# RoPE and per-head scores on one core: which loads of q GpSimd issues around DMA engine 4

## The chip, the cores and the metric

The kernel runs on one core of a Trainium2 chip. The metric is device time in microseconds (us), the median of several executions; a profile of one further execution shows where the time lies. A core has TensorE (PE; its weight loads are listed as PEld), VectorE (DVE), ScalarE (ACT), GpSimd (POOL) and SyncE (SP, which only issues DMAs here), and 16 DMA engines that move data between HBM and the core's SBUF.

## The reference

q and k have 16 batches of 512 positions, 16 heads and 64 values, in float32. Each is rotated by its position's cos and sin, and then the scores of every pair of positions are taken, per batch and head:

```python
q_rot = np.concatenate([q1 * cos_q - q2 * sin_q, q1 * sin_q + q2 * cos_q], axis=-1)
k_rot = np.concatenate([k1 * cos_q - k2 * sin_q, k1 * sin_q + k2 * cos_q], axis=-1)
scores = np.einsum('bshd,bthd->bsht', q_rot, k_rot)
```

The inputs are 67 MB together, the output is 268 MB.

## The kernel before

Position s of a batch lies at partition s // 4 and chunk s % 4, so a batch of q or k is a tile of 128 partitions by 16 KB, and each partition's 16 KB are contiguous in HBM. A step handles one chunk of q of one batch: 64 steps, i = 0 to 63, four per batch. In a step, for each of eight pairs of heads p, TensorE multiplies the transposed q chunk with the batch's transposed k (`scores`, line 392), ScalarE copies the result from PSUM into a stage tile (line 418), and after the eighth pair SP stores the stage, 4 MB, in one DMA (line 427, recorded in the profile at line 237, that of the helper `dma`). There are three stages; a stage is filled again when its store has landed. Between the pairs TensorE transposes the q chunk of the next step and the k chunk of the step four later (`transposed`, line 349), and VectorE rotates q two steps ahead and k five steps ahead (`rope`, line 312). The first batch is treated in smaller pieces and stored in 16 DMAs of 1 MB.

q and k have two input buffers each, so batch b of q uses the buffer of batch b - 2. Its load is placed at the end of step i with i % 4 == 2, as batch i // 4 + 2 (lines 507 and 508): the load of q13 at the end of step 46, q14 of step 50, q15 of step 54. k's load follows at the end of the next step, two batches and more ahead (k15 at the end of step 51). After the load of q15, in step 54, nothing is left to load, and steps 55 to 63 only store.

Every operation is added to a plan (`Plan.add`), which works out the semaphore waits, and each engine's queue holds its operations in the plan's order. SP's queue thus holds stores and loads in the order of the steps, each behind the one before it.

`load` (line 264) has two forms. A plain load is one DMA of 128 partitions issued by SP. The batches listed in `RELIEVED` (line 260) are loaded in another way: GpSimd resets the cursor of its own DMA queue (line 107), moves it by a tiny DMA (`move_cursor`, line 282) of 5 rows, so that the next transfer begins behind engine 4 (`SLOW`), and then issues a load of the first 120 partitions (`halves`, line 289), which is meant for the other 15 engines, eight partitions each in two pieces of 8 KB a partition. The last 8 partitions depend on the entry's number x. With x even, SP loads them by a DMA of 8 rows, a row to each of eight engines, engine 4 among them. With x odd, GpSimd loads them first, with a cursor moved by 8, so that they are meant for the other eight engines. GpSimd has no other work after the start, so its queue waits only for the input buffer to be free: until VectorE and TensorE have read batch b - 2 to its end.

The function that the diff touches holds the whole kernel; its part around the change is the dictionary `RELIEVED` and `load`, and the loop over the steps calls it.

Of the kernel before, what the change touches and what calls it, by code (L numbers as in the profile page):

```python
# [178 lines left out]
def kernel(  # L179
# [56 lines left out]
    def dma(engine, e, dst, src, sem, reads=(), writes=(), also=()):  # L236
        plan.add(engine, one(lambda: e.dma_start(dst, src)), reads, writes, sem=sem, also=also)  # L237
# [19 lines left out]
            writes=[("unit", which, u) for u in us], also=[x for u in us for x in unit_keys(which, u)],  # L257
        )

    RELIEVED = {("q", 5): 0, ("q", 8): 1, ("q", 11): 2, ("q", 14): 3}  # L260
    tiny = [0]
    SLOW = 4

    def load(which, b):
# [5 lines left out]
        rest = [("in rest", which, b % 2, c) for c in range(C)]  # L270
        if (which, b) not in RELIEVED:
            dma(SP, nc.sync, t.rearrange("p c (h d) -> p c h d", h=H), dram[which][b], sem, writes=rows + rest)
# [5 lines left out]
        n, E, F = 120, C * H * D, C * H * D // 2  # L278
        x = RELIEVED[which, b]
        d = dram[which][b]  # L280
# [266 lines left out]
```

## Time and profile before

| | |
|---|---|
| median of 7 runs | 799.02 us (798.49 to 801.58) |
| profiled execution | 798.86 us, span 797.0 us |
| PE busy | 684.2 us (86%) |
| ACT busy | 562.7 us (71%) |
| DVE busy | 545.3 us (68%) |
| POOL busy | 8.5 us (1%) |
| DMA | 335.87 MB, mean 421 GB/s over the span |
| HBM read, written | 67.24 MB, 268.44 MB |
| loads of q by SP (plain) | 2048 KB, 29.2 us from issue to landing |
| loads of q by GpSimd (four) | 1920 KB, 32.7 us from issue to landing |

Busy shares are means over the span. A DMA's time from issue to landing holds its time in the queues of the DMA engines behind earlier DMAs. A DMA raises its semaphore once for each of the 16 engines, and the trace keeps the times of these 16 landings, without the engine's number; it also keeps the start, length and size of every packet.

### The profile page before, as it was taken

The numbers are of one execution on the slowest core, as the hardware profiler recorded it, in microseconds if no ns is written. First come the engines' busy times: TensorE is split into PE (matmuls) and PEld (weight loads), VectorE is DVE, ScalarE is ACT, GpSimd is POOL, SyncE is SP. The second block draws the span as 40 slices with busy tenths as digits, with TensorE's granted clock in tenths as the row PEclk, the third lists the DMA queues.
The fourth block names the chain that finished last, engine by engine and source line by source line (L and its number), as shares of the span: only waits on it lengthen the run. The fifth ranks groups of instructions, "written<-read, shape, count | busy, mean of one in ns | idle before, by whom it ended". The sixth has DMA issues, their size and how long they took to land.

```text
span 797.0 us, 8197 instructions
## 1 busy us (share of the span) xinstructions
PE 684.2 (86%) x3072; PEld 295.3 (37%) x3072; DVE 545.3 (68%) x516; ACT 562.7 (71%) x647; POOL 8.5 (1%) x18
## 2 busy tenths in 40 slices
PE   4989999897988979799797988979879799899960
PEld 2444443342433434343343433434334344344320
DVE  6999988575775867667585866858758478586300
ACT  2978886775866858578685856868757677678760
POOL 0000000000000000100000000000000100000000
PEclk9999999998997989989999989999989899899995
DMA  8999999999999999999999999999999999999995
GB/s 347 422 424 430 433 407 439 423 437 425 428 423 428 426 442 422 434 430 407 433 430 435 431 433 431 421 429 434 429 428 432 433 423 417 427 437 433 430 433 232
DMA packets 18513, 335.87 MB, mean 421 GB/s; under 512 B 2128, under 2 KB 3408, under 8 KB 4432
## 3 DMA queue, kind: packets, MB, share of 16 engines
q1 hardware_dynamic: 16832, 327.42, 96.4%
q0 software_dynamic: 1376, 8.13, 2.5%
q10 hardware_dynamic: 288, 0.13, 0.1%
q8 instruction: 6, 0.10, 0.0%
q14 instruction: 11, 0.09, 0.0%
HBM read 67.24 MB, written 268.44 MB: 421 GB/s over the span
## 4 chain that ended last, share of the span: by engine, by line
DMA 47%; PE 38%; DVE 6%; ACT 5%; issue 0%; ACTq 0%; DVEq 0%; SPq 0%
DMA out_dram<-st 47%; PE ps L409 28%; PE bank L360 9%; ACT st L418 5%; DVE part L335 2%; DVE st L335 2%; DVE k_sb L335 1%; DVE q_sb L335 1%; DMA st<-in_k_dram 1%; DVE kT L378 0%; DVE qT L378 0%; ACTq L110 0%; DVEq L110 0%; SPq L542 0%; SPq L513 0%
## 5 line engine op out<-in xcount | busy, mean ns | idle before, releaser
L418 ACT COPY st<-ps 128x1024 f32<-128x1024 f32 x512 | 495.8, 1018 | 197.9 <-DMA out_dram<-st 110.0
L409 PE MATMUL ps<-kT,qT 64*128 64x512 f32 x2048 | 543.4, 646 | 73.9 <-ACT st L418 73.9
L409 PEld LDWEIGHTS ps<-kT,qT 64*128 64x128 f32 x2048 | 182.1, 195 | 264.2 <-issue 134.8
L378 DVE COPY qT<-bank 128x512 f32<-128x512 f32 x118 | 81.6, 692 | 197.1 <-PE bank L360 197.1
L360 PEld LDWEIGHTS bank<-ident,q_sb 128*128 128x128 f32 x480 | 54.4, 149 | 101.1 <-issue 96.8
L360 PE MATMUL bank<-ident,q_sb 128*128 128x128 f32 x480 | 85.1, 304 | 1.0 <-DVE q_sb L335 1.0
L360 PEld LDWEIGHTS bank<-ident,k_sb 128*128 128x128 f32 x480 | 50.5, 141 | 93.7 <-DVE k_sb L335 45.7
L360 PE MATMUL bank<-ident,k_sb 128*128 128x128 f32 x480 | 78.7, 287 | 1.2 <-DVE qT L378 0.8
L378 ACT COPY kT<-bank 128x512 f32<-128x512 f32 x122 | 72.4, 597 | 6.7 <-PE bank L360 6.7
L335 DVE TENSOR_TENSOR part<-q_sb,ss_t 128x1024 f32<-128x1024 f32 x60 | 73.5, 1225 | 3.2
L335 DVE TENSOR_TENSOR k_sb<-k_sb,part 128x1024 f32<-128x1024 f32 x60 | 73.5, 1225 | 2.1
L335 DVE TENSOR_TENSOR q_sb<-q_sb,cos_t 128x1024 f32<-128x1024 f32 x60 | 73.5, 1225 | 2.1
L335 DVE TENSOR_TENSOR k_sb<-k_sb,cos_t 128x1024 f32<-128x1024 f32 x60 | 73.5, 1225 | 2.0
L335 DVE TENSOR_TENSOR part<-k_sb,ss_t 128x1024 f32<-128x1024 f32 x60 | 73.0, 1216 | 0.3
L335 DVE TENSOR_TENSOR q_sb<-q_sb,part 128x1024 f32<-128x1024 f32 x60 | 72.9, 1216 | 0.0
L360 PE MATMUL bank<-ident,st 128*128 128x128 f32 x64 | 10.7, 318 | 12.7 <-DVE st L335 12.7
L360 PEld LDWEIGHTS bank<-ident,st 128*128 128x128 f32 x64 | 8.3, 161 | 18.0 <-DVE st L335 17.0
L335 DVE TENSOR_TENSOR part<-st,ss_t 128x1024 f32<-128x1024 f32 x8 | 9.8, 1223 | 5.9 <-DMA st<-in_k_dram 5.5
L335 DVE TENSOR_TENSOR st<-st,part 128x512 f32<-128x512 f32 x16 | 11.1, 691 | 0.5
L237 POOL DMA_DIRECT2D scratch<-in_q_dram x6 | 3.6, 602 | 615.4 <-PE bank L360 615.4
L335 DVE TENSOR_TENSOR st<-st,cos_t 128x1024 f32<-128x1024 f32 x8 | 9.8, 1225 | 0.3
L378 ACT COPY qT<-bank 128x512 f32<-128x512 f32 x10 | 5.7, 615 | 3.5 <-PE bank L360 3.5
(11 smaller groups left out, 11.0 us busy)
## 6 DMA issues: line engine op xcount, KB each, us to landing
out_dram<-st SPq DMA_DIRECT2D x60, 4096.0 KB, 25.2
k_sb<-in_k_dram SPq DMA_DIRECT2D x15, 2048.0 KB, 27.2
q_sb<-in_q_dram SPq DMA_DIRECT2D x11, 2048.0 KB, 29.2
out_dram<-st SPq DMA_DIRECT2D x16, 1024.0 KB, 12.6
q_sb<-in_q_dram POOLq DMA_DIRECT2D x4, 1920.0 KB, 32.7
st<-in_k_dram SPq DMA_DIRECT2D x1, 1536.0 KB, 8.8
st<-in_q_dram SPq DMA_DIRECT2D x1, 1536.0 KB, 12.0
st<-in_k_dram SPq DMA_DIRECT2D x1, 512.0 KB, 4.5
```

The lines of the kernel that those rows point to most:

```text
L237: plan.add(engine, one(lambda: e.dma_start(dst, src)), reads, writes, sem=sem, also=also)
L335: plan.add(DVE, one(lambda: nc.vector.tensor_tensor(o, a, b, op=op)), reads, writes, also=more)
L360: done = [nc.tensor.transpose(bank[:, x, :], srcs[x], ident) for x in range(4)]
L378: plan.add(engine, one(lambda: copy(out=dst, in_=src)), [("bank", m)], keys)
L409: nc.tensor.matmul(out=ps[:, r, :], lhsT=lhs[lo:hi, :], rhs=rhs[lo:hi, :], start=True, stop=True)
L418: plan.add(ACT, one(lambda: nc.scalar.copy(out=so, in_=si)), [("ps", y)], [("st", s, p)])
```

## The change

The batch q14 leaves the list of relieved loads, and q13 and q15 join it. There are five such loads instead of four. q13 takes the number 3, the odd form that q14 had; q15 takes the number 4, the even form of q5 and q11. q14 becomes a plain load by SP. Nothing else is changed.

```diff
-    RELIEVED = {("q", 5): 0, ("q", 8): 1, ("q", 11): 2, ("q", 14): 3}
+    RELIEVED = {("q", 5): 0, ("q", 8): 1, ("q", 11): 2, ("q", 13): 3, ("q", 15): 4}
     tiny = [0]
     SLOW = 4
```

The lines of `load` that read it:

```python
        if (which, b) not in RELIEVED:
            dma(SP, nc.sync, t.rearrange("p c (h d) -> p c h d", h=H), dram[which][b], sem, writes=rows + rest)
            return
...
        plan.add(POOL, None, (), rows)
        if x % 2:
            move_cursor(8)
            halves(n, P, rest, f"rest{x}")
        move_cursor(SLOW + 1)
        halves(0, n, rows, f"part{x}")
        if not x % 2:
            dma(SP, nc.sync, t[n:].rearrange("p c (h d) -> p c h d", h=H), d[n:], sem, writes=rest)
```

## The prediction

> **What bounds the kernel now.** I read four views: the windows by stage, the chain of work that ended last, the waits, and then, because they point at the DMA engines, the trace's packet and landing records.
>
> The windows' columns are the stretch, its length, busy time (instructions) of PE, PEld, DVE, ACT and POOL, the clock, the DMA engines' mean busy share and GB/s:
>
> ```profile
> 600.00:700.00 100.00, 90.54 (x396) 38.61 (x392) 70.04 (x66) 71.74 (x83) 2.48 (x4) 0.91 1.01 427
> 700.00:780.00 80.00, 67.47 (x308) 28.59 (x304) 34.49 (x35) 59.40 (x66) 0.00 (x0) 0.96 1.00 433
> 780.00:797.00 17.00, 0.00 (x0) 0.00 (x0) 0.00 (x0) 0.00 (x0) 0.00 (x0) 0.50 0.46 197
> ```
>
> The 16 DMA engines are full up to 780 us, while every compute engine has idle time. In the last 17 us they are 46% busy: some have finished, others have not. That is the only DMA time left to win. The chain that ended last and the waits from 690 us on say who paces whom:
>
> ```profile
> 744.15 21.47 DMA out_dram<-st
> 765.62 0.02 issue
> ...
> 770.37 2.72 ACT st L418 x3
> 773.09 0.07 issue
> 773.17 1.03 ACT st L418
> ```
>
> ```profile
> ACT st L418 <- DMA out_dram<-st: 10.7, 6, 2.7
> ```
>
> A store's landing frees a stage buffer, ACT fills it, the next store is issued. The last store is issued at 774.22 and lands 20.57 us later, though an engine's share of one store takes 9.68: it stands in a queue. So the end is the moment when the last engine has worked off its queue, not when ACT finishes.
>
> Each DMA's semaphore records 16 landings, one per engine. I sorted those of three stores (us; from the landing records):
>
> ```
> store 54 (issued 676.02)   first 693.88 ... 14th 698.64  15th 699.57  last 700.97
> store 59 (issued 735.01)   first 747.08 ... 14th 751.90  15th 752.84  last 755.70
> store 63 (issued 774.22)   first 785.80 ... 14th 790.62  15th 791.55  last 794.79
> ```
>
> Fifteen engines keep their distances; one falls behind, from 1.40 behind the 15th to 3.24. Packets can be strung engine by engine (each starts within 0.01 us of the end of the one before it, with no holes), and the strings show why: fifteen need 9.68 us for a store, this one 9.86 to 10.01 (its 32 KB packets take 1.23 to 1.26 us, the others' 1.21). It is also the one string without 8 KB packets in the loads of q5 and q11: engine 4. Its lag at the end, 3.24 us, is the most that relieving it alone could give.
>
> **The change, part by part.** Durations are from the profiled execution: 798.86 us with a span of 797.0, so 1.86 us around it; it stands 0.16 below the median of 799.02.
>
> (1) q15 leaves SP's queue and goes to POOL. These rows are what is removed (the second, store 55 and those after it, follows in the queue) and the nearest model of what is added, the load of q11, which has the same even form:
>
> ```profile
> 676.39 0.86 SPq L237 DMA_DIRECT2D q_sb<-in_q_dram  x1
> 693.24 81.32 SPq L237 DMA_DIRECT2D out_dram<-st  x9
> ```
>
> ```profile
> 475.70 0.58 POOL L237 DMA_DIRECT2D scratch<-in_q_dram  x1 [146.57 <-PE bank L360]
> 476.29 0.75 POOL L237 DMA_DIRECT2D q_sb<-in_q_dram  x1
> ```
>
> Issue costs are hidden: POOL gains a cursor reset, a tiny DMA (0.58) and a load (0.75) with nothing queued behind it; SP swaps an issue of 0.86 for that of the 8-row remainder, 17 us ahead of its next store. POOL waits until q13's last transposes have read the buffer, a wait that SP's load met too, but POOL does not stand behind store 54. It will issue near 670:
>
> ```profile
> 669.06 0.66 PE L360 MATMUL bank<-ident,q_sb 128*128 128x128 f32 x4
> ```
>
> By q11 (issued 476.29, remainder landed about 508.7) q15 is in by about 703. DVE reads it first at 711.46, so that cover is 8 us; beyond it, each us late would be a us of DVE.
>
> ```profile
> 711.46 1.23 DVE L335 TENSOR_TENSOR part<-q_sb,ss_t 128x1024 f32<-128x1024 f32 x1
> ```
>
> (2) What counts is work per engine. A plain load is 4.86 us on each (8 packets of 16 KB at 0.61). In the even form (by the strings of q11, where eight show a single 16 KB packet) engine 4 keeps one of eight packets; seven others take it on top of their full share (+0.61), eight take just their share. By bytes engine 4 wins 4.25. What it won in fact, from the strings: q5 and q11 each lie in a run of one load and four stores, which plainly costs 4.86 + 4 x 9.68 = 43.58, and on engine 4 4.87 + 4 x 9.95 = 44.67.
>
> ```
>                        engine 4                        last of the other fifteen
> around q5     179.69 to 222.69 = 43.00 (-1.67)    179.69 to 224.04 = 44.35 (+0.77)
> around q11    475.16 to 517.50 = 42.34 (-2.33)    473.80 to 518.04 = 44.24 (+0.66)
> ```
>
> Engine 4 gives back 2 to 2.5 of its 4.25: its stores last about 11.3 us while the others mix the two queues. So q15 puts engine 4's end at 794.79 - 1.67 to 2.33, or 792.5 to 793.1, and the next one's at 791.55 + 0.66 to 0.77, or 792.3. Engine 4 stays last, barely.
>
> (3) The k load after each relief was slow too: 5.97 and 6.17 us on engine 4, 6.55 and 5.62 on the other, against 4.86. After q15 no load follows, only stores, so I cost this at nothing; were it paid in another form, up to 1.3 would go on engine 4 and 1.7 on the other.
>
> (4) The fourth relief moves from q14 to q13, one batch earlier, the odd form in both. Landing to landing, with the k load after it, q8 and q14 took 48.67 and 48.11 on engine 4 against a plain 4 x 9.95 + 2 x 4.87 = 49.54: -0.87 and -1.43. Bounds: a loss of 0.56 (q13 gives what q8 gave) to a gain of about 0.5 (relief varies as much upwards). I take a loss of 0.2, nearer q14, its neighbour. q14 as a plain load must be in by 664.2, when DVE reads it; behind store 50 (landed 654.77) plus 4.86 it lands about 659.7, as it did by POOL.
>
> Sum: 794.79 - 2.0 + 0.2 = 793.0, a gain of 1.8: 797.2 against the median of 799.02.
>
> **A rule against the change.** The row first: in the strings the next packet begins as the last one ends, the whole way. The Trainium skill, "DMA: Bandwidth & Descriptors" (section "Rules for kernel authors"), says that spreading DMAs over issuing engines doesn't help, since all run on the same 16, and that splitting a transfer by partitions is no use. By it the change wins 0, and the page's fixed cost of some 2.0 us per DMA ("Anatomy of one DMA"), if exposed, would make it 2 us slower. It counts all 16 as equals; these rows show one that is not, and no hole in which a fixed cost could stand.
>
> **The rivals.**
>
> Given back: engine 4's relief is eaten by contention. Counted to the end of the k load, q5 and q11 won engine 4 only about 0.5 and 1.0 while the other lost up to 2.4; then the end lies at 793.8 to 794.6, a gain of 0.2 to 1.0: 798.0 to 798.8. For it: loads slow down in every such batch. Against: here the slow load doesn't exist. Chance 0.26, with a landing of the relief on the wrong engine (about 799) in it at 0.02; the two strings without 8 KB packets speak against that.
>
> Slower: the last store comes too late. q15's transfers now mix with stores 53 and 54 and delay their landings by up to 4.86, and so the filling for stores 56 and 57. Compute goes at 10.02 a step there (stores at 693.24, 703.26, 713.28), the DMA at 9.68, so a delay is not caught up. Price: on empty engines a store needs 9.68 plus about 3.3 (a 512 KB load landed 4.5 after its issue, 1.2 of it data), so an issue later than 794.79 - 13.0 = 781.8 costs its lateness. The worst here is 774.22 + 4.86 = 779.1. It decides only if another 2.7 come from somewhere, and 4.3 for 0.2%: some 800.8. Chance 0.10.
>
> **How the numbers follow.** The forecast has 0.64, with gains of 1.2 (the lower relief, the whole loss of step 4) to 2.6 (engine 4 no longer last: 791.55 + 0.66). 0.2% of 799.02 is 1.6 us, about what a measurement of this kernel can tell from no change; the forecast of 1.8 lies close to that line. Faster: the four fifths of the forecast that lie beyond 1.6, 0.52. Same: its rest and "given back", 0.38. Slower: 0.10. Range 796.2 to 799.0: from that upper end, less 0.2 for the spread of the runs, to the end of "given back", more 0.2.
>
> **What would show it.** In the profile after: POOL loads of q13 near 573 and of q15 near 670; the last store landing about 1.8 us earlier after a like issue; the share in the last stretch higher; landings of the last store with a gap behind the 15th of 0 to 1.3 instead of 3.24. It is wrong if another engine ends beyond 793.5, if engine 4's stores after 700 take over 10.0, or if DVE waits for q15.

## The result and the profile after

The changed kernel takes 797.04 us (median of 17 runs) against 798.82 us (median of 40 runs of the kernel before): 1.8 us less. The ratio is 0.998, with a 95% interval of 0.9971 to 0.9989. The forecast was 797.2. The profiled execution took 796.57 us with a span of 794.8.

The first view is GpSimd's part of the timeline (start, length, instruction), from the fourth relieved load on, then SyncE's:

```profile
572.06 0.59 POOL L237 DMA_DIRECT2D scratch<-in_q_dram  x1 [95.25 <-PE bank L360]
572.65 0.57 POOL L237 DMA_DIRECT2D q_sb<-in_q_dram  x1
573.21 0.57 POOL L237 DMA_DIRECT2D scratch<-in_q_dram  x1
573.78 0.76 POOL L237 DMA_DIRECT2D q_sb<-in_q_dram  x1
669.43 0.58 POOL L237 DMA_DIRECT2D scratch<-in_q_dram  x1 [94.89 <-PE bank L360]
670.01 0.75 POOL L237 DMA_DIRECT2D q_sb<-in_q_dram  x1
```

```profile
626.91 0.90 SPq L237 DMA_DIRECT2D q_sb<-in_q_dram  x1
...
675.45 0.93 SPq L237 DMA_DIRECT2D q_sb<-in_q_dram  x1
693.55 77.79 SPq L237 DMA_DIRECT2D out_dram<-st  x9
```

The change is there as written: q13 by GpSimd in four DMAs (the odd form), q15 in two, q14 by SyncE at 626.91, and at 675.45 only the 8-row remainder of q15. The windows (columns as before) and the end of the chain that ended last:

```profile
700.00:780.00 80.00, 66.30 (x308) 27.70 (x305) 34.80 (x35) 59.52 (x67) 0.00 (x0) 0.96 1.01 433
780.00:797.00 17.00, 0.00 (x0) 0.00 (x0) 0.00 (x0) 0.00 (x0) 0.00 (x0) 0.51 0.45 195
```

```profile
743.48 20.00 DMA out_dram<-st
763.47 0.02 issue
...
763.55 5.93 ACT st L418 x7
769.48 0.41 issue
769.88 1.09 ACT st L418
```

The DMA engines are still full to 780 us, and the work after it is the same (45% of 17 us, 7.7 us an engine, against 7.8): the average engine ends when it did before. What is gone is the wait for the last one. The 16 landings of the last store, from the trace's records, tell it for both kernels:

```
          issued   first    14th     15th     last     mean of 16
before    774.22   785.80   790.62   791.55   794.79   788.68
after     771.00   785.99   791.35   791.96   792.50   788.69
```

The mean has not moved by more than 0.01 us; the last landing comes 2.29 us earlier. Strung packet by packet, engine 4 is now the 15th, at 791.96 (it still loses 0.25 to 0.34 us per store from store 55 to store 60, and goes from 4.55 behind the first in store 55 to 5.97 in store 61). Last is an ordinary engine, one of the seven that took a row of q15's remainder, and it keeps its distance to the first to within 0.3 us over the last nine stores. A second profile of the changed kernel (797.16 us, "the changed kernel itself" below) shows the same order: engine 4 is the 15th at 792.85, an ordinary engine the last at 793.09.

### The profile page after: what moved, and what is told of

Same layout as the page of the kernel before. It is cut to its first block, busy times and chain, and to the rows that moved or that the text cites. A ratio compares the mean times of both kernels' runs of the same rounds, so it can differ in the third digit from the quotient of the medians.

```text
span 794.8 us, 8200 instructions
## 1 busy us (share of the span) xinstructions
PE 681.4 (86%) x3072; PEld 293.9 (37%) x3072; DVE 545.3 (69%) x516; ACT 562.2 (71%) x647; POOL 9.8 (1%) x20
## 4 chain that ended last, share of the span: by engine, by line
DMA 48%; PE 36%; DVE 6%; ACT 6%; issue 1%; ACTq 0%; DVEq 0%; SPq 0%
DMA out_dram<-st 48%; PE ps L409 27%; PE bank L360 9%; ACT st L418 5%; DVE part L335 2%; DVE st L335 2%; DVE k_sb L335 1%; DVE q_sb L335 1%; DMA sin_t<-in_sin_dram 0%; DVE kT L378 0%; DVE qT L378 0%; ACTq L237 0%; ACT ss_t L455 0%; ACT ss_t L454 0%; ACTq L110 0%
## 6 DMA issues: line engine op xcount, KB each, us to landing
out_dram<-st SPq DMA_DIRECT2D x16, 1024.0 KB, 13.5
```

## The experiments

All are the changed kernel with one edit. Times are medians, and ratios are against the kernel before, run on the same chip. The last store's landings are those of each one's single profiled execution, which can lie off its median: "no relief" was profiled at 806.31 us, 2.0 above its median, "all odd" at 796.05, 1.2 below.

```
                          first    14th     15th     last     mean
move only                 786.93   792.06   792.29   795.14   789.37
add only                  786.15   791.68   792.32   794.08   789.23
q15 on all 16             787.01   791.40   791.47   794.38   789.33
q15 odd form              786.43   791.34   791.95   792.04   789.08
around engine 12          785.62   790.99   791.13   795.41   788.87
no relief                 794.08   798.12   798.58   802.40   795.34
k15 instead of q15        790.56   794.96   795.74   795.97   792.90
all odd                   785.94   790.87   791.65   791.99   788.85
```

### The two parts apart

```diff
-    RELIEVED = {("q", 5): 0, ("q", 8): 1, ("q", 11): 2, ("q", 13): 3, ("q", 15): 4}
+    RELIEVED = {("q", 5): 0, ("q", 8): 1, ("q", 11): 2, ("q", 13): 3}                # move only
+    RELIEVED = {("q", 5): 0, ("q", 8): 1, ("q", 11): 2, ("q", 14): 3, ("q", 15): 4}  # add only
```

> Four relieved loads, q5, q8, q11 and q13; q14 and q15 are plain. Theory (the queue of engine 4 sets the end): in the changed kernel engine 4 landed k15 at 670.69 against 671.16 before, so without a relief of q15 it ends about 0.5 us ahead of before, at most 0.4 behind it: 798.3 to 799.2, the last store's lag behind the 15th landing about 3. Rival (the gain comes from the earlier place of the fourth relief): most of the 1.8 us is here, 797.0 to 797.4.

> Five relieved loads, q5, q8, q11, q14 and q15. Theory: the fifth relief alone carries the gain; engine 4 ends at 792.3 to 792.8, the next one at 792.3, so 2.0 to 2.5 us under before: 796.3 to 796.8. Rival (the place of the fourth relief carries it): no change from before, 798.8.

Moving alone: 798.91 us, ratio 1.0 (0.999 to 1.0009), and the last landing is again 2.85 us behind the 15th. Adding alone: 797.21 us, ratio 0.9976 (0.9957 to 0.9995). The fifth relief carries the gain and the move carries none of it; the time of adding alone is 0.4 us above the range expected. The single profile of "add only" (798.16 us, above its median) ends with an ordinary engine at 794.08 and engine 4 near 792.3, as the theory put engine 4; how far back the last ordinary engine lies differs from one execution to the next by more than the forecast allowed.

### Is it engine 4, or the issue by GpSimd?

```diff
         plan.add(POOL, None, (), rows)
+        if x == 4:                                   # q15 on all 16
+            halves(0, P, rows + rest, f"part{x}")
+            return
...
-        move_cursor(SLOW + 1)
+        move_cursor(13 if x == 4 else SLOW + 1)      # around engine 12
```

> As the changed kernel, but GpSimd loads q15 in one DMA of 128 partitions over all 16 engines, in the same 8 KB pieces and at the same place: it leaves SP's queue and mixes with the stores, but engine 4 has its full share. Theory (it is the bytes that engine 4 is spared): the gain is gone, engine 4 ends at 794.3 plus 0 to 2 us for the mixing: 798.3 to 800.5. Rival (it is the issue by GpSimd, ahead of SP's queue): the gain stays, 797.0 to 797.4.

> As the changed kernel, but the tiny DMA ahead of q15 has 13 rows in place of 5, so that the load of its 120 partitions goes around engine 12; engine 4 gets its full share and a row of the remainder. Theory (only engine 4's queue matters): the gain is lost, and engine 4 has 0.61 us more than with four reliefs, plus 0 to 0.7 for the mixing: 799.5 to 800.3. Rival (any engine left out, or the issue by GpSimd in this form, does it): 797.0.

On all 16 engines: 799.51 us, ratio 1.0007 (0.9998 to 1.0016). Around engine 12: 799.48 us, ratio 1.0009 (1.0 to 1.0018). In both, q15 leaves SyncE's queue at the same place and in the same 8 KB pieces, and nothing is gained. The last landing is 2.9 and 4.3 us behind the 15th: engine 4 is last again. So the gain is the bytes that engine 4 is spared: sparing engine 12 in its place brings none.

### No relief at all

```diff
-    RELIEVED = {("q", 5): 0, ("q", 8): 1, ("q", 11): 2, ("q", 13): 3, ("q", 15): 4}
+    RELIEVED = {}
```

> All loads plain. Theory (a relief followed by another load nets engine 4 about 0.7, 0.9, 1.15 and 1.43 us, as worked out from the kernel before, far less than the 4.2 to 4.9 us of its bytes): 4.2 us over the kernel before, 802.3 to 803.8, and engine 4 far behind the 15th landing, by 8 or more. Rival (the bytes count in full): 18 us over before, 815 to 818. Rival (contention gives all of it back): 798.8 to 799.5.

804.34 us, ratio 1.0064 (1.0051 to 1.0078): 5.3 us over the kernel before, 0.5 beyond the upper end of the first expectation and far from both rivals. The lag was expected wrongly: engine 4 is 3.8 us behind the 15th landing, not 8 or more, because the others are held back too (below). So the four reliefs of the kernel before are worth about 1.3 us each on average, and the fifth, from "move only" to the changed kernel, 1.9. Its windows:

```profile
100.00:700.00 600.00, 529.89 (x2336) 226.00 (x2332) 416.70 (x390) 425.09 (x488) 0.00 (x0) 0.93 1.00 425
700.00:780.00 80.00, 74.66 (x336) 32.42 (x336) 39.28 (x39) 63.17 (x71) 0.00 (x0) 0.96 0.97 416
780.00:810.00 30.00, 0.79 (x4) 0.00 (x0) 0.00 (x0) 1.89 (x2) 0.00 (x0) 0.66 0.48 209
```

Here the DMA share falls to 0.97 already before 780: the buffers come free at engine 4's pace, 8.3 us behind the first, and the others run dry. The last store shows it: 11 of its 16 landings lie within 0.2 us of the first. In this kernel those engines wait for their work, instead of working it off at their own distances.

### The place of the relief

```diff
-    ... ("q", 13): 3, ("q", 15): 4}
+    ... ("q", 13): 3, ("k", 15): 4}
```

> The fifth relief goes to k15 (even form) in place of q15; the plain load of q15 follows it and is the last load. Theory (the load that follows a relief gives part of it back): engine 4 nets only 0.7 to 1.15 against four reliefs (798.9), and the last ordinary engine pays 1.4 to 2.4: 797.5 to 798.5. Rival (a relief is worth the same anywhere near the end): 796.8 to 797.3.

800.04 us, ratio 1.0013 (1.0004 to 1.0022): slower than before, and about 1 us slower than with four reliefs ("move only"). Both expectations were too low. The same relief, one load earlier, costs more than it saves: by the landings engine 4 ends at 794.96, 0.2 us before its end in "move only" (0.7 to 1.15 had been expected), and the last ordinary engine at 795.97, 3.7 us later than there (1.4 to 2.4). GpSimd's rows of this kernel, and the windows over the loads, first of this kernel and then of the changed one:

```profile
643.35 0.58 POOL L237 DMA_DIRECT2D scratch<-in_q_dram  x1 [68.67 <-PE bank L360]
643.93 0.75 POOL L237 DMA_DIRECT2D k_sb<-in_k_dram  x1
```

```profile
640.00:664.00 24.00, 23.75 (x114) 10.42 (x114) 18.79 (x19) 20.27 (x25) 1.33 (x2) 1.00 1.00 383
664.00:700.00 36.00, 27.99 (x124) 11.95 (x120) 20.95 (x20) 22.03 (x26) 0.00 (x0) 0.86 1.00 428
```

```profile
640.00:664.00 24.00, 23.75 (x114) 10.34 (x115) 19.52 (x18) 19.98 (x23) 0.00 (x0) 1.00 1.00 429
664.00:700.00 36.00, 28.82 (x126) 12.33 (x126) 21.58 (x21) 22.95 (x26) 1.33 (x2) 0.91 1.01 433
```

Both kernels show the DMA engines full (1.00), but from 640 to 664 this one moves 383 GB/s and the changed one 429. k15's packets go in beside those of q14, a plain load still under way (issued at 627.04), and the packets of both loads take longer. Summed over the 16 engines, the time that load packets took beyond their usual 0.61 us (16 KB) and 0.31 us (8 KB) is:

```
                                            16 KB    8 KB
after, 548 to 625 (q13 relieved, then k14)  17.0     0.6
after, 625 to 668 (q14, k15 plain)           0.1     -
after, 668 to 712 (q15 relieved, last)       0.0     0.0
k15 instead, 625 to 690 (q14, k15)          25.0    12.7
k15 instead, 690 to 705 (q15 plain)          9.6     -
no relief, 100 to 700                       91.5     -
```

Of the 17.0 in the first row, 14.5 are k14's, right behind the relief, and 2.4 are q12's, ahead of it. A relieved load that mixes with no other is itself quick in this table; the plain load right behind it, or a load that it mixes with, is slowed. The other reliefs agree: in the kernel before, the k loads right behind the four reliefs lost 9.0, 13.5, 6.9 and 9.7 us, and the plain loads behind a plain load, from 250 us on, 0 to 1.9; in the changed kernel it was 7.3 to 15.5 against 0 to 2.4, with one plain load of 8.1. (Of the relieved loads, q14 of the kernel before lost 5.6, the others 0.6 or less.) The 47 us of "k15 instead" over 16 engines are 3 us each; the mean landing of its last store is 4.2 us later than in the changed kernel, and the rest is not accounted for. The last load has no load behind it and pays nothing.

### Where the remainder goes

```diff
-    ... ("q", 13): 3, ("q", 15): 4}
+    ... ("q", 13): 3, ("q", 15): 5}                                                     # q15 odd form
+    RELIEVED = {("q", 5): 1, ("q", 8): 3, ("q", 11): 5, ("q", 13): 7, ("q", 15): 9}     # all odd
```

> As the changed kernel, but q15 takes the odd form: its last 8 partitions go by GpSimd to the eight engines without engine 4. Theory (an ordinary engine of the eight that took a row of the remainder is now last, at 792.50 against 791.96 for engine 4): both lose the 0.61 us of that row, the last landing is near 791.9 and the time 0.4 to 0.7 us under the changed kernel: 796.3 to 796.6. Rival (the two further DMAs of the odd form cost as much as they save): no change from 797.0, or up to 0.5 more.

> All five relieved loads in the odd form, so that the rows that the fifteen leave over go five times to the eight engines without engine 4, which end 2 to 6 us before the last. Theory: engine 4 and its seven neighbours lose the three rows of q5, q11 and q15, 1.8 us against the changed kernel, some of it given back by the k loads that follow q5 and q11: 795.5 to 796.6, under both kernels. Rival (what the odd form adds in DMAs and mixing, or the other eight, set the end): 796.7 to 797.5.

q15 in the odd form: 796.72 us, ratio 0.998 (0.9971 to 0.9989). All five in it: 797.25 us, ratio 0.9981 (0.9971 to 0.9991). The first came out 0.1 us above its expectation and the second 0.65 above its own, inside the range of its rival: the three rows saved should have brought up to 1.8 us, and the time is that of the changed kernel. The landings say why. With q15 alone in the odd form engine 4 is last, at 792.04; with all five it ends at 790.87, so on engine 4 the rows saved at q5 and q11 did bring 1.2 us. But two ordinary engines now end behind it, at 791.65 and 791.99, and their strings hold 18 or more pieces of 8 KB of q15 where engines without a remainder have 16: they are of the eight that take the remainder. So the other eight set the end, as the rival had it. This rests on one profile of each kernel.

To see whether the odd form for q15 is better than the changed kernel, both ran once more on one chip:

> The changed kernel itself, beside the next one on the same chip: 796.5 to 797.5.

> The odd form for q15 once more, now beside the changed kernel on the same chip. Theory (the 0.61 us of a row fewer on the engines that end last): 0.3 to 0.6 us under it. Rival (no gain, the first difference was chance): within 0.2 us of it.

796.98 us (ratio 0.9974, 0.9963 to 0.9984) and 796.63 us (0.9973, 0.9964 to 0.9982). The odd form is 0.35 us under the changed kernel, as in the first round (0.32), but the intervals lie on each other: it is clearly better than the kernel before, and not shown to be better than the changed one.

### What slows engine 4

```diff
         def tt(o, a, b, op, reads, writes):                                          # small rope
+            if n >= C:
+                o, a, b = o[:, :1], a[:, :1], b[:, :1]
...
+        N = S if i < 1 else 64                                                       # short matmuls
...
-                    nc.tensor.matmul(out=ps[:, r, :], lhsT=lhs[lo:hi, :], rhs=rhs[lo:hi, :], start=True, stop=True)
+                    nc.tensor.matmul(out=ps[:, r, :N], lhsT=lhs[lo:hi, :], rhs=rhs[lo:hi, :N], start=True, stop=True)
```

(In the first, the swapped operand of the sum is cut to one head to match.)

> As the changed kernel, but from the second batch on VectorE rotates only the first heads' columns of each chunk (the rest of q and k goes into the scores unrotated): VectorE's work falls to a small part, every DMA stays. Question: what makes engine 4's 32 KB store packets take 1.23 to 1.26 us while the others take 1.21? If VectorE's work does it, engine 4's stores go down to 9.68 us in mid-run; if not, they stay at 9.9 to 10.0. Time within 2 us of the changed kernel either way.

> As the changed kernel, but from step 1 on each scores matmul computes 64 of its 512 columns (the rest of the scores is what PSUM held): the count of instructions stays, TensorE's time in them falls to about an eighth, every DMA stays. If TensorE's streaming slows engine 4, its stores go down to 9.68 us in mid-run; if not, they stay at 9.9 to 10.0. Time within 2 us of the changed kernel.

One run each: 796.34 and 796.98 us. The engines' lines of the two pages, the first of "small rope", the second of "short matmuls":

```profile
PE 678.8 (85%) x3072; PEld 293.7 (37%) x3072; DVE 182.0 (23%) x516; ACT 561.9 (71%) x647; POOL 9.8 (1%) x20
```

```profile
PE 556.1 (70%) x3072; PEld 424.8 (53%) x3072; DVE 540.5 (68%) x516; ACT 544.3 (68%) x647; POOL 9.8 (1%) x20
```

DVE's busy time falls from 69% to 23%, PE's from 86% to 70%, and engine 4 doesn't notice. (PE's time was to fall further: a scores matmul has an eighth of its columns, but the granted clock of this run is 0.52 in place of 0.94, and a matmul takes 0.44 us on average in place of 0.64.) Between 705 and 760 us, 6.4% and 5.7% of all 32 KB packets take over 1.216 us, with a mean of 1.26; in the changed kernel 6.4%, mean 1.26 (one engine in 16 is 6.25%). From 775 us on, when compute is over, none does, in any of the three. By these two runs, how much VectorE or TensorE computes is not the cause. The number of instructions was the same in all three, and ScalarE's work was not cut; what slows engine 4 stays open.

## Why the prediction was right, and where it was off

**What bounds it.** Right, and shown: taking relief off engine 4 ("no relief") costs 5.3 us, giving its full share back while all else stays ("all 16", "engine 12") takes the whole gain away.

**Step 1, the issue.** Right. GpSimd issued q15 at 670.01, behind q13's last transposes. Its last part landed at 705.49 (estimated 703), and VectorE read it first at 712.26, so 6.8 us of cover were left of the 8. q14, plain, landed at 656.2.

**Step 2, the work per engine.** In the changed kernel's strings the run around q15 took engine 4 from 670.28 to 712.41, 42.13 us, 2.54 under the plain 44.67, where q5 and q11 had given 1.67 and 2.33. The last ordinary engine took 670.33 to 714.70, 44.37, 0.79 over its 43.58 (0.66 to 0.77 had been put down). The method held; engine 4's own relief was sized 0.2 to 0.9 too low.

**Step 3, no load behind.** Right, and the step on which the size of the gain rests. The excess of load packets after 668 us is 0.0, against 14.5 in k14, right behind q13. The rival "given back" had its mechanism right (the k15 experiment shows it at work) and the place wrong.

**Step 4, q13 for q14.** Inside its bounds, on the other side of the value taken. Around q13 engine 4 took 47.95 us, 1.59 under plain, better than q14's 1.43; it landed k15 at 670.68, 0.48 earlier than before, where a loss of 0.2 was taken.

**The sum.** Engine 4 was to end at 793.0, barely last; it ended at 791.96, and the ordinary engine, put at 792.3, ended at 792.50 and took over the end. Two terms of engine 4 were wrong, the relief (0.5 too small) and the move (0.7 too late); together they put its end 1.0 too late, which did no harm, since the second queue stood right behind. The span of the profiles fell 2.2 us, the medians 1.8: that the medians met the forecast to 0.1 is in part luck. The lowest gain of the forecast, 1.2, is 1.1 by its own terms (1.67 less 0.56). One of the forecast's signs of being wrong came up by the letter: engine 4 took 10.02 us for store 57. That says nothing against the change, since it took 10.00 for the same store in the kernel before.

**The rule against the change.** The rule (the Trainium skill, "DMA: Bandwidth & Descriptors", "Rules for kernel authors") that spreading over issuing engines and splitting by partitions does not help holds, in these runs, where the load keeps its share on every engine: on all 16 the same GpSimd issue brought nothing. It did not hold for sparing the one slow engine, which was worth 1.9 us. No exposed fixed cost of 2 us was seen: the GpSimd issue on all 16 stands 0.6 us above "move only".

**The rival on the other side.** It had the last store issued later; it was issued at 771.00, 3.2 us earlier. 2.2 us of that is the landing that frees its buffer, that of store 60, which no longer waits for engine 4 (763.47 in place of 765.62); from there to the issue it was 7.5 us in place of 8.6. "After a like issue" in the forecast's list of signs was wrong in the same way. The share in the last stretch did not rise either (0.45 against 0.46): the window had a fixed end, and the mean work left was the same.

## What to carry to other kernels

When the DMA engines are full to the end, look at the 16 landings of the last transfers: the time to win is the distance from the last to the next, then to the mean (here 3.2 and 6.1 us), and here only bytes taken off the last engine won it. Rebalance in the last load, behind which no other load runs, because a load behind it, or beside it, takes back part of the gain, or all of it. And put what the slow engine is spared on engines that end early, not on the one that will be last next.

## What had not been expected

A full DMA share says nothing of how much is moved: with k15 relieved, the share stayed at 1.00 while 383 GB/s were moved instead of 429. Loads also lose time without any relief: in "no relief" the 16 KB packets lost 91.5 us between 100 and 700, summed over the engines. The engines run close together there, but that this is the reason is not shown. And relieving a load where it overlaps with another made the kernel slower (800.04 us), though the same bytes were moved off the slow engine.
